# The last block's window units in another order, the samples' two in the middle, and the samples' norm on another engine

## Chip, cores and metric

One core of a Trainium2 chip runs the whole kernel. The metric is the device time of one execution in microseconds (us), the median of three runs. The engines are TensorE (PE, matmuls), VectorE (DVE), ScalarE (ACT) and GpSimd (POOL); SyncE (SP) issues DMAs from a queue that it works through in order, as every engine works through its own instructions in order.

## What is computed

One inference step of a two-layer encoder on a prompt of 1024 frames and 8 samples of 16 frames, width 1024. The parts that the change touches, cut from the reference:

```python
# layer 0: RWKV-7 time mixing, then a SwiGLU FFN; layer 1: attention, then a SwiGLU FFN
y, wkv_new = wkv7_scan(r, decay, k, v, -kk, kk * a_gate, wkv_prev)   # wkv_prev: the samples' states
y = (y - mu) * rsqrt(var + LNX_EPS) * ln_w + ln_b + bonus            # per head
out = (y * g) @ w_o                                                   # output projection
x = x + gate * out
h = rms_norm(x, g) * (1 + scale) + shift                              # before each FFN, K/V and Q
x = x + gate * (silu(h @ w_gate) * (h @ w_up)) @ w_down
```

`shift`, `scale` and `gate` are one vector for the prompt and one for each of the 8 samples ("modulations", themselves matmuls of the condition with a large weight).

## The kernel before

The 1152 columns (1024 prompt frames, 128 sample frames) are held as three blocks of 384. The scan runs by **windows** of 128 columns, 9 of them, and each window by two halves of the heads. One window and one half is a **unit**: number 12 is window 6, first half, 13 its second half, up to 17. Units 16 and 17 are window 8, which holds the samples; they start from the states read from memory (`ssv`, the tiles `sv` in the code, two buffers, one for each half of the samples) and write 16 new states back (`um`, `s2`, then a store). Units 12 to 15 carry the state `S` from window to window, so that 14 needs 12's result and 15 needs 13's; 16 and 17 need nothing of the others.

A unit has four steps: `win_prep` (loads `XL`, `BK`, `UV`, first products `G`), `win_run` (a chain of small matmuls: `st`, then `xs`, `TT`, then `Y`, which closes it), `win_post` (centre, variance, scale of `y`, ending in a store of the unit's `y` to the block `yg`), and a next unit's `win_prep`. `windows` runs the post of a unit beside the run of the next.

`outproj(b, c0, c1)` is the output projection of a column range of a block: it reads `yg` back (`mr`), splits it into a high and a low part (`mx` on ACT, the rest on DVE, line 255), does for each of 8 output tiles three matmuls per pair of tiles (24 matmuls `acc`, the weight `raw` also split into `whi` and `wlo`), adds the residual (`e`) and sums squares (`sqa`). Each matrix product in the kernel is done as these three matmuls. `outproj(2, 0, 256)` needs the units 12 to 15, `outproj(2, 256, 384)`, the samples' columns, the units 16 and 17. `ada` yields pieces of the modulations' product.

The program is written by Python generators: `alternate(a, b, m, n)` takes m steps of one and n of the other. A list scheduler then orders each engine's instructions, with the written order as priority.

After the last `outproj`, the first FFN begins (`S<-h,w`). It works in two column groups, c = 0 (512 prompt columns) and c = 1 (512 prompt and 128 sample columns). `strassen_in` loads the 8 tiles of a group, norms them (`normed`: DVE, line 326, and ACT, line 327), splits them (`h`) and forms sums of them on POOL (line 1230). The 128 sample columns are normed by `normed_samples`, three operations on a 128x128 tile, in four places: first FFN, K/V, Q, second FFN. The c = 0 part takes the memory that the units' pool frees (`cw.close()`).

Of the kernel before, what the change touches and what calls it, by code (L numbers as in the profile page):

```python
# [11 lines left out]
ALU = mybir.AluOpType  # L12
# [125 lines left out]
def mm(nc, out, lhsT, rhs, start, stop):  # L138
    return nc.tensor.matmul(out, lhsT, rhs, start=start, stop=stop)  # L139


class Trunk:
# [186 lines left out]
    def normed_samples(self, t, x, r, A, sh0, f):  # L329
        nc = self.nc  # L330
        tv = t.rearrange("p (b n) -> p b n", b=8)
        bc = lambda v: v[:, 1:9].rearrange("p (b o) -> p b o", o=1).broadcast_to([128, 8, 16])
        gp = nc.gpsimd
        gp.tensor_tensor(t, x, r, ALU.mult)
        gp.tensor_tensor(tv, tv, bc(A[:, f]), ALU.mult)
        gp.tensor_tensor(tv, tv, bc(self.mod[:, sh0 + f]), ALU.add)


    def proj_open(self, ctx):
# [364 lines left out]
    def win_open(self, ctx):  # L704
        nc = self.nc
        self.wp = ctx.enter_context(self.tc.tile_pool(name="win", bufs=1, reuse_waits="tile"))

        self.T = self.wp.tile([128, 16, 16], F32, name="T")
        nc.sync.dma_start(self.T.rearrange("p c i -> p (c i)"), self.a["ti"])
        self.Z = [self.dp.tile([64, 32, 64], F32, name=f"Z{i}") for i in range(2)]  # L710
        z = self.wt("y", [128, 512])
        nc.gpsimd.memset(z, 0.0)
        for i in range(2):
            zf = self.Z[i].rearrange("c g i -> (c g i)").rearrange("(u p x) -> u p x", u=2, p=128)
            for u in range(2):
                nc.sync.dma_start(zf[u], z)
        flat = lambda t: t.rearrange("p a b c d -> p (a b c d)")
        self.early = [lambda: flat(self.wt("YL", [128, 2, 2, 4, 64], 2))] * 2 + \
            [lambda: self.wt("BKT", [128, 2, 2, 256], 2).rearrange("p a b c -> p (a b c)")] * 2 + \
            [lambda: self.wt("XL", [128, 3, 8, 64], 2).rearrange("p a b c -> p (a b c)")] * 2 + \  # L720
            [lambda: self.wt("BK", [128, 8, 2, 64], 1).rearrange("p a b c -> p (a b c)"),
             lambda: self.wt("pa", [128, 2, 8, 64], 1).rearrange("p a b c -> p (a b c)")]
        self.zr = self.wp.tile([128, 128], F32R, name="zr")
        nc.scalar.activation(self.zr, z[:, 0:128], AF.Copy)
        self.eends = [self.wp.tile([128, 8, 12], F32, name=f"eend{b}") for b in range(NB)]
        self.S = []
        for h in range(2):
            s = self.wp.tile([128, 4, 64], F32, tag=f"S{h}", name=self.nm("S"), bufs=3)
            nc.gpsimd.memset(s, 0.0)
            self.S.append(s)  # L730
# [276 lines left out]
    def win_post(self, w, hf, R):  # L1007

        nc = self.nc
        b, wi = divmod(w, 3)  # L1010
        fs = slice(4 * hf, 4 * hf + 4)
        gt = self.wt("gl", [128, 512], 1)
        nc.sync.dma_start(gt.rearrange("p (f t) -> p f t", f=4), self.sp[b]["g"][:, wi, fs, :])
        bv = self.wt("bv", [128, 512], 1)
        nc.sync.dma_start(bv.rearrange("p (f t) -> p f t", f=4), self.sp[b]["v"][:, wi, fs, :])
        bn = self.wt("bn", [128, 512], 1)
        nc.sync.dma_start(bn.rearrange("p (f t) -> p f t", f=4), self.sp[b]["bn"][:, wi, fs, :])
        nc.gpsimd.tensor_tensor(bv, bv, bn, ALU.mult)
        y = self.wt("y", [128, 512], 1)
        nc.scalar.activation(y, R.Y, AF.Copy)  # L1020
        cen = self.bank("st", 2)
        mm(nc, cen, self.C("cen"), y, True, True)
        nc.scalar.activation(y, cen, AF.Square)
        yield
        var = self.bank("st", 2)
        mm(nc, var, self.C("bo"), y, True, True)
        nc.scalar.activation(y, var, AF.Ln, bias=self.eps[:, 1:2], scale=1.0 / 64)
        nc.scalar.activation(y, y, AF.Exp, scale=-0.5)
        nc.vector.tensor_tensor(y, cen, y, ALU.mult)
        yield  # L1030
        for f in range(4):
            s = slice(f * 128, (f + 1) * 128)
            nc.vector.scalar_tensor_tensor(y[:, s], y[:, s], self.P("lnw", 4 * hf + f), bv[:, s], ALU.mult, ALU.add)
        for f in range(4):
            s = slice(f * 128, (f + 1) * 128)
            nc.vector.scalar_tensor_tensor(y[:, s], y[:, s], self.P("lnb", 4 * hf + f), gt[:, s], ALU.add, ALU.mult)
        nc.scalar.dma_start(self.yg[b][:, fs, wi * 128:(wi + 1) * 128], y.rearrange("p (f t) -> p f t", f=4))

    @staticmethod
    def weave(*gens):  # L1040
# [100 lines left out]
    def layer0a(self, ctx):  # L1141
        self.yg = [self.dp.tile([128, 8, TB], F32, name=f"yg{b}") for b in range(NB)]
        c1, cw, ct = ExitStack(), ExitStack(), ExitStack()
        self.ps = c1.enter_context(self.tc.tile_pool(name="psA", bufs=1, space=PSUM, reuse_waits="tile"))
        self.win_open(cw)
        with ExitStack() as c2:
            self.proj_open(c2)
            for _ in self.proj(0):
                pass
            for b in range(1, NB):  # L1150
                w = self.windows([(w, hf) for w in range(3 * b - 3, 3 * b) for hf in range(2)])
                for _ in self.alternate(w, self.proj(b), 5, 4):
                    pass
        self.tail_open(ct)
        self.nraw, self.nhi, self.nlo = (2, 2, 2)
        self.nmix, self.nmr = 16, 2

        def ada():
            while next(self.ada, StopIteration) is not StopIteration:
                yield  # L1160

        def early():
            for b in range(2):
                yield from self.outproj(b)
        units = lambda t: self.windows([divmod(int(x), 2) for x in t.split()])
        for _ in self.alternate(units("12 13 14 15"), self.alternate(ada(), early()), 1, 1):
            pass
        for _ in self.alternate(units("16 17"), self.outproj(2, 0, 256), 3, 1):
            pass
        cw.close()  # L1170
        for _ in self.outproj(2, 256, 384):
            pass
        ct.push(c1)
        return ct.close
# [740 lines left out]
```

## Time and profile before

| | |
|---|---|
| median of three runs | 3966.8 us (3949.72, 3966.8, 3968.19) |
| profiled execution | 3959.5 us |
| its span, first to last instruction | 3957.6 us (1.9 us lie around it) |
| mean granted TensorE clock | 0.924 of full speed |
| PE busy | 3572.2 us, 90% of the span |
| DVE, ACT, POOL busy | 58%, 40%, 18% of the span |

The span is the time from the first to the last instruction in the trace; all times below count from its start. The profiled execution is 7.3 us under the median. A granted clock of 1.00 is 2.4 GHz, of 0.50 is 1.2 GHz; a stretch between them spent a part of its time at either.

### The profile page before, as it was taken

What the parts mean: (1) busy time and instruction counts of PE and PEld (TensorE: products, weight loads), DVE (VectorE), ACT (ScalarE), POOL (GpSimd) and SP (SyncE); (2) the same over time, 40 slices, a digit from 0 to 9 for tenths busy, and PEclk for the clock granted to TensorE, in tenths of its full rate; (3) what the DMA queues carried; (4) which work ended last, traced back from release to release, by engine and by line L of the source; (5) the groups of instructions that cost most, each with busy time, mean ns of one, the idle gap of its engine ahead of it and who ended that gap; (6) DMA issues with size and microseconds to landing.
All of it is one profiled execution on the core that took longest, in us unless ns stands there. A gap on an engine that the chain in (4) does not pass through costs nothing. (4 is left out here: it accounts for less than half of the span.)

```text
span 3957.6 us, 72834 instructions
## 1 busy us (share of the span) xinstructions
PE 3572.2 (90%) x28814; PEld 3153.8 (80%) x28814; DVE 2284.7 (58%) x4263; ACT 1586.3 (40%) x2994; POOL 708.6 (18%) x635
## 2 busy tenths in 40 slices
PE   6878998888887889999999999888889789999999
PEld 4766776776775679999988888777677789999998
DVE  4475575475554575455455852566676665545567
ACT  5554565363322343333321253455554443333310
POOL 0110110020000065454200200100000265444000
PEclk8888898798887769999999999999999889999999
DMA  5785685668764422222655313254464422222522
GB/s 201 216 246 141 178 243 163 177 182 234 216 161 123 139 76 84 73 73 75 216 204 189 105 62 100 81 165 147 142 199 148 160 68 73 75 75 91 172 79 73
DMA packets 439478, 556.56 MB, mean 141 GB/s; under 512 B 128864, under 2 KB 304224, under 8 KB 434656
## 3 DMA queue, kind: packets, MB, share of 16 engines
q1 hardware_dynamic: 384992, 533.01, 43.1%
q10 hardware_dynamic: 54144, 18.89, 2.1%
q8 instruction: 227, 3.72, 0.4%
q14 instruction: 115, 0.94, 0.1%
HBM read 417.63 MB, written 134.12 MB: 139 GB/s over the span
## 5 line engine op out<-in xcount | busy, mean ns | idle before, releaser
L139 PE MATMUL S<-h,w 128*128 128x320 f32 (+1 forms) x4944 | 695.5, 300 | 12.2 <-DVE h L255 3.1
L139 PEld LDWEIGHTS S<-h,w 128*128 128x128 f32 x4944 | 676.1, 193 | 18.6 <-DVE h L255 7.0
L139 PE MATMUL acc<-mx,whi 128*128 128x384 f32 (+2 forms) x1856 | 558.1, 382 | 63.9 <-ACT mx L254 31.1
L139 PE MATMUL S<-h,wh 128*128 128x320 f32 (+1 forms) x2844 | 532.0, 338 | 12.0 <-DVE h L1107 5.7
L139 PEld LDWEIGHTS S<-h,wh 128*128 128x128 f32 x2844 | 457.0, 190 | 68.4 <-issue 12.6
L139 PEld LDWEIGHTS acc<-mx,whi 128*128 128x128 f32 x1856 | 386.3, 223 | 99.7 <-ACT mx L254 36.1
L254 ACT ACTIVATE w<-rq 128x512 fp32r<-128x512 f32 x308 | 192.2, 629 | 499.4 <-PE S L139 199.6
L255 DVE TENSOR_TENSOR w<-rq,w 128x512 fp32r<-128x512 f32 x308 | 270.9, 883 | 200.5 <-ACT w L254 199.1
L139 PE MATMUL PT<-h,w 128*128 128x320 f32 (+1 forms) x2448 | 354.0, 300 | 16.7 <-ACT w L254 6.3
L139 PE MATMUL acc<-mx,wlo 128*128 128x384 f32 (+2 forms) x928 | 347.0, 375 | 7.1 <-DVE wlo L255 7.0
L139 PEld LDWEIGHTS PT<-h,w 128*128 128x128 f32 x2448 | 336.7, 193 | 20.7 <-ACT w L254 6.5
L139 PE MATMUL PT<-h,wh 128*128 128x320 f32 (+1 forms) x1428 | 288.5, 345 | 8.6 <-DVE wh L255 3.9
L1300 POOL TENSOR_TENSOR t<-t,t 128x576 f32<-128x576 f32 (+1 forms) x132 | 214.9, 1628 | 414.6 <-ACT t L1307 295.7
L139 PEld LDWEIGHTS PT<-h,wh 128*128 128x128 f32 x1428 | 235.2, 191 | 38.3 <-issue 8.8
L255 DVE TENSOR_TENSOR wlo<-raw,whi 128x1024 fp32r<-128x1024 f32 x116 | 146.1, 1262 | 127.3 <-ACT whi L254 126.3
L139 PEld LDWEIGHTS acc<-mx,wlo 128*128 128x128 f32 x928 | 205.0, 221 | 15.9 <-DVE wlo L255 9.1
L254 ACT ACTIVATE whi<-raw 128x1024 fp32r<-128x1024 f32 x116 | 121.8, 1053 | 143.2 <-PE acc L139 82.2
L255 DVE TENSOR_TENSOR h<-h,h 128x1024 fp32r<-128x1024 f32 (+4 forms) x112 | 123.3, 1115 | 85.5 <-ACT h L254 70.6
L254 ACT ACTIVATE h<-h 128x1024 fp32r<-128x1024 f32 (+4 forms) x112 | 103.2, 934 | 166.6 <-DMA h<-sd 114.8
L254 ACT ACTIVATE wh<-rq 128x512 fp32r<-128x512 f32 x124 | 74.6, 625 | 230.8 <-PE S L139 145.0
L1300 DVE TENSOR_TENSOR t<-S,t 128x576 f32<-128x576 f32 (+1 forms) x116 | 86.4, 744 | 129.9 <-PE S L139 129.8
L1367 DVE TENSOR_TENSOR h<-h,S 128x640 f32<-128x640 f32 (+1 forms) x150 | 112.0, 750 | 79.7 <-PE S L139 79.3
(424 smaller groups left out, 5748.8 us busy)
## 6 DMA issues: line engine op xcount, KB each, us to landing
h<-in_wada SPq DMA_DIRECT2D x64, 512.0 KB, 6.0
rq<-in_wg SPq DMA_DIRECT2D x88, 256.0 KB, 2.6
rq<-in_wu SPq DMA_DIRECT2D x88, 256.0 KB, 2.6
rq<-in_wd SPq DMA_DIRECT2D x88, 256.0 KB, 3.0
raw<-in_wada SPq DMA_DIRECT2D x32, 512.0 KB, 5.0
raw<-in_rw_o SPq DMA_DIRECT2D x32, 512.0 KB, 4.3
kc<-in_ck SPq DMA_DIRECT2D x16, 1024.0 KB, 5.1
vc<-in_cv SPq DMA_DIRECT2D x16, 1024.0 KB, 5.9
```

The source lines that it names most:

```text
L139: return nc.tensor.matmul(out, lhsT, rhs, start=start, stop=stop)
L254: self.nc.scalar.activation(hi, x, AF.Copy)
L255: self.nc.vector.tensor_tensor(lo, x, hi, ALU.subtract)
L1300: eng.tensor_tensor(out, x, y, ALU.add)
L1367: nc.vector.tensor_tensor(y, y, d, ALU.add)
```

## The change

Three things are edited. `layer0a` runs all six units from one generator, in the order 12, 13, 16, 14, 15, 17 instead of 12, 13, 14, 15 and then 16, 17. Beside it, in the ratio two steps of units to one, run the modulations and the projections, now with `outproj(2, 0, 256)` at their end; a set `posted`, which `win_post` fills, holds that back until unit 15's post has been written. And `normed_samples` issues its three operations on VectorE instead of GpSimd (8 tiles in 4 places, 96 instructions).

```diff
-        gp = nc.gpsimd
-        gp.tensor_tensor(t, x, r, ALU.mult)
-        gp.tensor_tensor(tv, tv, bc(A[:, f]), ALU.mult)
-        gp.tensor_tensor(tv, tv, bc(self.mod[:, sh0 + f]), ALU.add)
+        dve = nc.vector
+        dve.tensor_tensor(t, x, r, ALU.mult)
+        dve.tensor_tensor(tv, tv, bc(A[:, f]), ALU.mult)
+        dve.tensor_tensor(tv, tv, bc(self.mod[:, sh0 + f]), ALU.add)
...
+        self.posted = set()
...
         nc.scalar.dma_start(self.yg[b][:, fs, wi * 128:(wi + 1) * 128], y.rearrange("p (f t) -> p f t", f=4))
+        self.posted.add((w, hf))
...
         def early():
             for b in range(2):
                 yield from self.outproj(b)
-        units = lambda t: self.windows([divmod(int(x), 2) for x in t.split()])
-        for _ in self.alternate(units("12 13 14 15"), self.alternate(ada(), early()), 1, 1):
-            pass
-        for _ in self.alternate(units("16 17"), self.outproj(2, 0, 256), 3, 1):
+            while (7, 1) not in self.posted:
+                yield
+            yield from self.outproj(2, 0, 256)
+        w = self.windows([divmod(int(x), 2) for x in "12 13 16 14 15 17".split()])
+        for _ in self.alternate(w, self.alternate(ada(), early()), 2, 1):
             pass
         cw.close()
         for _ in self.outproj(2, 256, 384):
```

How the instructions stand is shown at three places. The number behind a name is that of the buffer's allocation; a row is line, operation, output<-inputs, shape, repeats.

**TensorE, where unit 16 closes.** Before, the closing products `Y_12990` of unit 16 are followed by the projection `outproj(2, 0, 256)` (`acc_13078`, then four more tiles; 115 of its matmuls stand there, up to unit 17's first `ssv` product):

```order
L139 MATMUL Y_12990<-XL_12592,ssv_12658 64x16 x23
L139 MATMUL st_12896<-um_12897,BKT_12630 64x256
L139 MATMUL Y_12990<-XL_12592,ssv_12658 64x16 x3
L139 MATMUL st_12896<-um_12900,BKT_12630 64x256
L139 MATMUL Y_12990<-XL_12592,ssv_12658 64x16 x3
L139 MATMUL acc_13078<-mx_12777,whi_13074 128x256
L139 MATMUL acc_13078<-mx_12778,whi_13074 128x256
L139 MATMUL acc_13078<-mx_12777,wlo_13075 128x256
```

Of the change, unit 16 (`Y_11867`) closes into the first products of unit 15 (`G`, from `XL_12243`) and the start of unit 14 (`Y_12209`):

```order
L139 MATMUL Y_11867<-XL_11477,ssv_11543 64x16 x12
L139 MATMUL st_11767<-um_11768,BKT_11515 64x256
L139 MATMUL Y_11867<-XL_11477,ssv_11543 64x16 x2
L139 MATMUL G_12254<-XL_12243,BK_12244 128x128 x3
L139 MATMUL st_11767<-um_11771,BKT_11515 64x256
L139 MATMUL G_12254<-XL_12243,BK_12244 128x128
L139 MATMUL G_12267<-XL_12243,BK_12244 128x128 x4
L139 MATMUL st_11778<-um_11779,BKT_11515 64x256
L139 MATMUL Y_12209<-zr 128x512
L139 MATMUL st_11778<-um_11782,BKT_11515 64x256
```

The state updates `um` of unit 16 now stand among other units' work. No `acc` row stands between unit 13's start and unit 17's first `ssv` products: block 1's projection ends ahead of them, and `outproj(2, 0, 256)` begins inside unit 17, with 94 of its 192 matmuls behind the post of unit 17.

**SyncE's queue, the samples' states of unit 17.** Before, the two loads `ssv` stand among unit 16's eight stores `out_wkv_s`, the first behind the sixth of them, the second behind the seventh:

```order
L946 DMA out_wkv_s<-s_2173_12925 128x256
L1133 DMA rr_13601<-in_x 128x256
L247 DMA raw_13674<-in_rw_o 128x1024
L998 DMA ssv_13175<-in_wkv 128x4x256
L946 DMA out_wkv_s<-s_2184_12975 128x256
L1136 DMA x_108<-e_2261_13460 128x256
L1133 DMA rr_13666<-in_x 128x256
L247 DMA raw_13772<-in_rw_o 128x1024
L998 DMA ssv_13177<-in_wkv 128x4x256
```

Of the change, they come behind the last of those stores, beside unit 15's loads of `UV`:

```order
L947 DMA out_wkv_s<-s_1956_11813 128x256
L826 DMA UV_12302<-sp_v_107 64x256 x3
L947 DMA out_wkv_s<-s_1960_11824 128x256
L826 DMA UV_12302<-sp_v_107 64x256
L791 DMA BK_12589<-sp_b_90 64x8x64
L999 DMA ssv_12658<-in_wkv 128x4x256
L999 DMA ssv_12660<-in_wkv 128x4x256
```

In the program's order two units, 14 and 15, now lie between these loads' place and unit 17.

**VectorE, behind unit 17's post.** Before, the four late low parts `mx` of the samples' columns (from `mr_13750` on) stand among the first norm operations of the FFN's c = 0 part (line 326):

```order
L1036 SCALAR_TENSOR_TENSOR y_13616<-y_13616,par,gl_13609 128x128 x4
L255 TENSOR_TENSOR mx_13749<-mr_13750,mx_13748 128x128
L255 TENSOR_TENSOR mx_13755<-mr_13756,mx_13754 128x128
L326 SCALAR_TENSOR_TENSOR x_14112<-x_14112,mod,x_14111 128x512
L326 SCALAR_TENSOR_TENSOR x_14113<-x_14113,mod,x_14111 128x512
L255 TENSOR_TENSOR mx_13761<-mr_13762,mx_13760 128x128
L326 SCALAR_TENSOR_TENSOR x_14114<-x_14114,mod,x_14111 128x512
L326 SCALAR_TENSOR_TENSOR x_14115<-x_14115,mod,x_14111 128x512
L255 TENSOR_TENSOR h_14122<-x_14112,h_14121 128x256
L255 TENSOR_TENSOR mx_13767<-mr_13768,mx_13766 128x128
```

Of the change, the same four stand at the end of that part, 57 rows and more behind its first norm operation, among its last splits (`h`, `w`):

```order
L255 TENSOR_TENSOR w_14261<-rq_14231,w_14260 128x512
L255 TENSOR_TENSOR h_14128<-x_14119,h_14127 128x256
L255 TENSOR_TENSOR mx_13749<-mr_13750,mx_13748 128x128
L255 TENSOR_TENSOR w_14265<-rq_14235,w_14264 128x512
L255 TENSOR_TENSOR mx_13755<-mr_13756,mx_13754 128x128
L255 TENSOR_TENSOR w_14269<-rq_14237,w_14268 128x512
L306 SCALAR_TENSOR_TENSOR kk_13716<-aux_13713,kk_13716 128x256
L255 TENSOR_TENSOR mx_13761<-mr_13762,mx_13760 128x128
L307 SCALAR_TENSOR_TENSOR rms_13715<-kk_13716,rms_13715 128x256
L255 TENSOR_TENSOR mx_13767<-mr_13768,mx_13766 128x128
```

The samples' projection has 168 matmuls behind the first of these four: half of its first two tiles and the six others whole.

## Rows read from the trace of the kernel before

**Rows 1.** The page's parts 1 and 2: busy time; granted clock in 40 slices (tenths).

```profile
PE 3572.2 (90%) x28814; PEld 3153.8 (80%) x28814; DVE 2284.7 (58%) x4263; ACT 1586.3 (40%) x2994; POOL 708.6 (18%) x635
...
PEclk8888898798887769999999999999999889999999
```

**Rows 2.** Stretches of 50 us: busy us of each engine, granted clock, DMA share, GB/s.

```profile
1150.00:1200.00 50.00, 40.06 (x448) 28.83 (x444) 23.40 (x57) 16.09 (x32) 2.55 (x2) 0.88 0.63 168
1200.00:1250.00 50.00, 36.77 (x375) 29.41 (x376) 16.37 (x40) 12.00 (x22) 1.26 (x1) 0.70 0.45 135
...
1350.00:1400.00 50.00, 30.54 (x128) 27.20 (x126) 37.57 (x73) 25.95 (x58) 17.32 (x16) 0.56 0.44 137
1400.00:1450.00 50.00, 37.42 (x181) 32.56 (x181) 33.48 (x57) 22.41 (x49) 27.48 (x36) 0.67 0.29 95
```

**Rows 3.** Timeline of PE, units 13 to 15: start, us, names, times, idle before.

```profile
1175.25 1.97 PE L139 MATMUL Y<-XL,S 64*64 64x64 f32 x32
...
1205.94 1.15 PE L139 MATMUL Y<-XL,S 64*64 64x64 f32 x32
...
1218.85 0.48 PE L139 MATMUL Y<-YL,UV 128*64 128x64 f32 x2 [4.88 <-DVE UV L931]
...
1245.44 1.15 PE L139 MATMUL Y<-XL,S 64*64 64x64 f32 x32
```

**Rows 4.** Timeline of PE, units 16 and 17.

```profile
1262.82 0.80 PE L139 MATMUL acc<-mx,whi 128*128 128x256 f32 x2 [4.93 <-ACT mx L254]
...
1280.64 0.82 PE L139 MATMUL Y<-XL,ssv 64*64 64x16 f32 x6
...
1302.83 0.42 PE L139 MATMUL st<-ssv,xm 64*32 64x64 f32 x8
...
1333.35 1.03 PE L139 MATMUL Y<-XL,ssv 64*64 64x16 f32 x8
```

**Rows 5.** Timeline of SP's queue, the samples' states for unit 17.

```profile
1300.60 0.38 SPq L998 DMA_DIRECT2D ssv<-in_wkv  x1
```

**Rows 6.** Timeline of ACT, unit 17's store.

```profile
1357.46 0.37 ACTq L1037 DMA_DIRECT2D yg<-y  x1
```

**Rows 7.** Timeline of PE from unit 17's store to the FFN.

```profile
1361.98 0.91 PE L139 MATMUL acc<-mx,whi 128*128 128x128 f32 x3 [8.95 <-ACT mx L254]
...
1413.88 0.80 PE L139 MATMUL aux<-sqa,cst 128*128 128x128 f32 x2 [1.43 <-DVE sqa L284]
1416.24 5.07 PE L139 MATMUL S<-h,w 128*128 128x256 f32 x24 [1.56 <-DVE kk L306]
```

**Rows 8.** PE by form, 1360 to 1415: count, busy us, mean ns, idle before.

```profile
L139 PE MATMUL acc<-mx,whi 128*128 128x128 f32 x112 | 35.8, 418 | 15.3 <-ACT mx L254 10.9 <-DVE e L1111 3.7 <-DVE mx L255 0.7
L139 PE MATMUL acc<-mx,wlo 128*128 128x128 f32 x56 | 23.2, 419 | 5.7 <-DVE wlo L255 5.7
```

**Rows 9.** Timeline of DVE after unit 17's store.

```profile
1364.22 0.75 DVE L326 SCALAR_TENSOR_TENSOR x<-x,mod,x 128x512 f32<-128x512 f32 x1 [1.36 <-DMA x<-x]
...
1404.05 0.67 DVE L255 TENSOR_TENSOR w<-rq,w 128x512 fp32r<-128x512 f32 x1
```

**Rows 10.** POOL, line 334: count, ns min/median/max, first and last start.

```profile
L334 POOL TENSOR_TENSOR xm<-h,rms x16: 458/870/912, 2261.3 to 2528.1; 128x128 f32<-128x128 f32 x16
```

**Rows 11.** DVE by form, 1400 to 1470.

```profile
L255 DVE TENSOR_TENSOR h<-x,h 128x320 fp32r<-128x320 f32 x28 | 27.5, 1030 | 2.8 <-ACT h L254 2.8
...
L1300 DVE TENSOR_TENSOR t<-PT,t 128x320 f32<-128x320 f32 x2 | 1.0, 482 | 0.0
L1111 DVE TENSOR_TENSOR e<-acc,mod 128x128 f32<-128x128 f32 x3 | 0.9, 285 | 4.2 <-PE acc L139 4.2
```

**Rows 12.** Stretches of 50 us at the shared K/V and the second FFN.

```profile
2250.00:2300.00 50.00, 42.38 (x188) 34.55 (x187) 41.69 (x60) 22.91 (x45) 23.75 (x30) 0.90 0.20 72
...
3150.00:3200.00 50.00, 30.82 (x142) 27.58 (x143) 43.20 (x57) 26.68 (x56) 37.29 (x43) 0.66 0.28 96
```

## The prediction

> **What bounds the kernel now.** I read the page first. TensorE is busy for 90% of the span, and its granted clock is 0.8 to 0.9 in many slices [rows 1]. So time can be won where TensorE waits or runs below full clock, and both of that is seen best in the stretches of 50 us: in the tail of the first layer, from 1150 to 1450, it is busy 31 to 40 us of each 50 that are shown, at a clock of 0.56 to 0.88, while DVE and ACT are far from full but for 1350 to 1400, where DVE is busy for 37.6 us [rows 2]. TensorE there waits for chains, not for a full engine.
>
> Then I followed the chain in the order of time. The closing products of the units end at 1177.2 (13), 1207.1 (14), 1246.6 (15), 1281.5 (16) and 1334.4 (17) [rows 3, 4]: intervals of 29.9, 39.5, 34.9 and 52.9 us. Three things lengthen them. Unit 15 falls into the stretch 1200 to 1250, in which TensorE idles 13.2 us [rows 2], 4.88 of it in a single wait [rows 3]. In unit 16 TensorE stands 4.93 us at a projection matmul whose input is unit 15's output, read back and split [rows 4]; the unit's own products queue behind it. And unit 17 begins only at 1302.83, 21.3 us after unit 16 closed [rows 4], because the second load of its states was issued at 1300.60 [rows 5], when unit 16's last updates had given the buffer back. TensorE is not idle in that gap: the projection of the first 256 columns fills it.
>
> Behind unit 17 comes a tail that nothing fills. Its output is stored at 1357.46 [rows 6]; 8.95 us of waiting for the read-back; then the samples' projection alone, and the FFN's first product starts at 1416.24 [rows 7], 58.8 us after the store. Of that, 168 matmuls take from 1361.98 to 1412.45 (the aux row less its wait [rows 7]), 50.5 us; taking off the waits of [rows 8] without the first (15.3 + 5.7 - 8.95 = 12.0) leaves 38.4 us, 0.23 each, at a granted clock of 0.56 [rows 2], nearly all at 1.2 GHz.
>
> **The order of the units, first part: up to unit 17's store.** Up to unit 13's end nothing is removed, so I start at 1177.2. Every unit then stands without a projection beside it until unit 17.
> - Unit 16: 34.9 less the 4.93 of its wait and some 24 projection matmuls gives 24 to 26; I take 28, with its ends at 24 and 35, because chain waits that a projection had filled stay.
> - Unit 14: 29.9 as it stands, some of it modulations; 28 (26 to 31). Unit 16's state updates overlap with it.
> - Unit 15: 39.5 less the 13.2 of idle time, which the projections' weight loads share the stretch with; 26 (24 to 30).
> - Unit 17: from 1302.83 to 1334.4 it took 31.6 with two dozen projection matmuls inside; it keeps as many; 31 (27 to 33). Its states are loaded two units ahead, so the gap of 21.3 us is gone.
> - Post: 1357.46 - 1334.4 = 23.1 [rows 4, 6]; more projection lies between; 24 (22 to 26).
>
> The sum is 1177.2 + 28 + 28 + 26 + 31 + 24 = 1314, against 1357.5: **43 us earlier** (25 to 57).
>
> **Second part: from the store to the FFN.** Here the change pays. Before, `outproj(2, 0, 256)` was done by then. Now 94 of its matmuls follow, and the samples' last four inputs are split on DVE at the end of the FFN's c = 0 norm and splits. That DVE block has its own length: from the store it ran through its first norm at 1364.22 to its last split, which ended at 1404.7 [rows 9], 47.3 us. The same rows must run now, with the projection's own splits among them as before, so the last input stands ready at about 47 us (45 to 50), and the 94 matmuls fit beside it. Behind it, 168 matmuls: 38.4 us at the lower level as measured, 19 at twice the clock. DVE is free by then and they can run densely, so I take 28. From the last matmul to the FFN's first product it took 1416.24 - 1412.45 = 3.8 [rows 7]. In all 47 + 28 + 3.8 = 79 us (68 to 92), against 58.8: **20 us paid back** (9 to 33). The 168 are the same number as in the old tail; the difference is that then they ran beside the DVE block, and now half behind it.
>
> Together: -43 + 20 = **-23 us**, with ends at 1300 + 68 = 1368 (-48) and 1332 + 92 = 1424 (+8).
>
> **The clock.** Same 32 closing products take 1.97 us in unit 13 and 1.15 in units 14 and 15 [rows 3]: the small matmuls do run at either level, and what stands beside a unit decides. The Trainium skill ("TensorE: Matmul & The Clock Gate", section "HAM oscillation — how this bites in real kernels") says that a TensorE which alternates between short bursts and waits falls back to its lower clock, and asks for matmuls to be kept together; by it taking the projections away from 16, 14 and 15 is the wrong direction, and the upper ends above would be the time. The trace agrees in part: unit 13 ran at the lower level though modulations stood beside it.
>
> **The norm of the samples' columns.** 24 operations in each of four places leave POOL and come to DVE. On POOL one took 0.46 to 0.91 us [rows 10]. On DVE the same shape takes 0.285 [rows 11], in all 6.8 us a place. Beside POOL, DVE is slower: a 128x320 split with both inputs in its memory took 1.03 us in the stretch where POOL works, against 0.48 for one with an input from PSUM [rows 11], a factor of 2.1; so up to 0.6 us, 14.4 a place. The Trainium skill ("SBUF — State Buffer", section "Who interferes with whom") has a rule for it: a DVE operation with two SBUF inputs and a POOL operation that reads SBUF shut each other out; the rows agree, and by it the moved operations cost the upper price wherever POOL's sums run beside them.
> What it hides behind: in the first FFN's stretch DVE has 16.5 us free of 50 [rows 2], at the second FFN 6.8, at K/V 8.3 [rows 12]; Q lies in a stretch where TensorE is nearly full. For POOL it is relief: its sums (line 1230), which the later splits wait for, come up to 24 operations earlier. At K/V and the second FFN, DVE goes over its free time by at most 6.1 + 7.6 us. Against that stand the 19.2 us that TensorE idles in the second FFN's stretch, some of which earlier sums may give back. I take 0, with ends -8 and +10. The scheduler also moves some attention work; no engine's amount changes, and I count nothing.
>
> **The rivals.**
> - *The clock comes back.* Dense matmuls behind the last input run at the upper level (19 us) and the units take their lower ends: -48. For it: unit 14 and 15's closing products at full speed; against: the old tail at 0.56. 3966.8 - 48 = 3919. Chance 0.25.
> - *The bare units and the tail stay at 1.2 GHz.* Upper ends: store at 1332, 79 to 85 more: 1411 to 1417, so -5 to +1, about 3964. For it: 0.56 and 0.67 in [rows 2]. Chance 0.26.
> - *The norm makes it slower.* All 96 operations at 0.6 us are 58 us of DVE. TensorE pays where DVE is the last to deliver, and DVE is at 41.7 and 43.2 of 50 at two of the four places [rows 12]. It decides the sign when more than 43 us of the 58 lie on the path (23 to eat the gain, 20 beyond); with all 58, -23 + 58 = +35, about 4002. Against it: free DVE time at the first FFN and at Q. Chance 0.14.
> - That the reorder does nothing because the scheduler undoes it: the order of the instructions excludes it.
>
> **How the numbers follow.** The forecast, chance 0.35: 3959.5 - 23 = 3936.5 on the profiled execution, and 7.3 more on the median, 3944; its own range is -36 to -10, 3931 to 3957. A measurement of this kernel tells about 0.5%, 20 us, from no change: faster is under 3947, slower over 3987. Faster: the first rival and some six tenths of the forecast, 0.25 + 0.21 = 0.46. Slower: the third, 0.14. The same: the second and the rest of the forecast, 0.26 + 0.14 = 0.40. The range for 8 in 10 leaves out the slower rival and a few in a hundred below: from -50 with the norm's -3 to the second rival with the norm's +10 and some more, 3914 to 3980.
>
> **What would show it.** In the profile after: unit 17's store near 1314 (under 1300 or over 1332 breaks the first part); no gap between a unit's close and the next unit's first products; unit 17's state loads issued a unit earlier; the FFN's first product near 1393, and TensorE waiting in the samples' projection for DVE's `mx`, 40 us and more after the store. If it doesn't wait there, the second part is wrong. The granted clock between 1177 and 1290 says which of the first two rivals holds. For the norm: TensorE's idle time in the four stretches against now, and the start of POOL's sums. The prediction is wrong as a whole if unit 15 or 17 waits for a load behind unit 16's stores in SP's queue, or if the change in the tail is given back in the FFN.

## The result, and the profile after

| | before | after |
|---|---|---|
| median, 12 runs each, side by side | 3955.05 us | 3975.99 us |
| lowest to highest | 3949.0 to 3968.45 | 3969.36 to 3984.86 |
| profiled execution | 3959.5 us | 3977.51 us |

The ratio is 1.0048, with a 95% interval of 1.0033 to 1.0064: the change makes the kernel slower by 19 us (13 to 25), just inside the 0.5% that the prediction calls "the same", but clear of zero, and on the other side of the forecast of 23 us faster. The measured 3975.99 us does lie in the range that the prediction gave, 3914 to 3980, but by luck: that range was counted from 3966.8, a median of three runs, and the 12 runs side by side with the change give 3955.05.

The page of the kernel after, its first two parts (busy time of each engine, then the span in 40 slices, in tenths):

```profile
span 3975.7 us, 72851 instructions
...
PE 3585.0 (90%) x28814; PEld 3152.8 (79%) x28814; DVE 2297.2 (58%) x4359; ACT 1588.0 (40%) x2994; POOL 658.7 (17%) x539
...
PE   6878888888898789999999999888889799999999
...
PEclk8988998798886769999999999989999889999999
```

The 96 norm instructions have gone from POOL to DVE. The counts say nothing about the loss, so the reading goes to the stretch that the order touches, cut at the closes of the units. After, one row for each of unit 16, 14, 15, 17, then unit 17's post up to its store, then from the store to the FFN's first product:

```profile
core 0: us, PE busy (x) PEld busy (x) DVE busy (x) ACT busy (x) POOL busy (x), PEclk, DMA share, GB/s
1172.50:1218.40 45.90, 42.63 (x448) 28.67 (x446) 15.56 (x41) 7.35 (x14) 1.27 (x1) 0.69 0.27 76
1218.40:1261.30 42.90, 38.15 (x274) 27.10 (x274) 19.41 (x50) 8.08 (x16) 1.27 (x1) 0.50 0.34 99
1261.30:1277.10 15.80, 11.01 (x168) 8.23 (x168) 4.29 (x13) 4.87 (x10) 1.26 (x1) 0.87 0.35 97
1277.10:1310.50 33.40, 30.87 (x393) 23.20 (x393) 11.25 (x29) 5.58 (x12) 1.27 (x1) 0.79 0.15 43
1310.50:1339.70 29.20, 25.21 (x142) 16.67 (x142) 19.23 (x47) 9.84 (x17) 0.00 (x0) 0.83 0.56 167
1339.70:1426.20 86.50, 61.14 (x292) 56.71 (x292) 52.68 (x101) 36.54 (x80) 20.09 (x16) 0.56 0.43 142
sum 253.70, PE 209.01 PEld 160.58 DVE 122.42 ACT 72.26 POOL 25.15; mean PE 34.83 PEld 26.76 DVE 20.40 ACT 12.04 POOL 4.19
```

The same windows of the kernel before, cut in the same way from the closes in [rows 3, 4] and the store in [rows 6]: units 14, 15, 16, the gap ahead of unit 17, unit 17, its post, and the way to the FFN:

```profile
1177.20:1207.10 29.90, 23.79 (x267) 17.16 (x267) 12.79 (x32) 8.06 (x16) 1.26 (x1) 0.81 0.55 155
1207.10:1246.60 39.50, 26.91 (x267) 21.82 (x267) 13.92 (x34) 10.23 (x19) 1.26 (x1) 0.70 0.45 130
1246.60:1281.50 34.90, 28.15 (x425) 21.11 (x425) 20.17 (x46) 9.51 (x18) 1.26 (x1) 0.84 0.40 114
1281.50:1302.80 21.30, 21.30 (x132) 17.01 (x132) 13.02 (x27) 6.09 (x9) 0.00 (x0) 0.94 0.50 158
1302.80:1334.40 31.60, 30.25 (x399) 23.15 (x399) 13.47 (x33) 7.36 (x14) 1.26 (x1) 0.85 0.41 128
1334.40:1357.50 23.10, 16.84 (x50) 8.65 (x50) 12.03 (x35) 3.63 (x8) 0.00 (x0) 0.65 0.17 52
1357.50:1416.20 58.70, 39.17 (x170) 37.10 (x170) 42.28 (x82) 28.10 (x64) 17.32 (x16) 0.50 0.38 119
sum 239.00, PE 186.41 PEld 146.00 DVE 127.68 ACT 72.98 POOL 22.37; mean PE 26.63 PEld 20.86 DVE 18.24 ACT 10.43 POOL 3.20
```

Read the two sums first. From unit 13's close to the FFN, 239.0 us have become 253.7, 14.7 us more. The two profiled executions are 18 us apart; -4.7 us lie ahead of unit 13's close and +8.1 us behind the FFN's first product. Among the other traces here both of these parts scatter by more than that: where the work ahead of it is left alone, unit 13 closes at 1170 to 1191 us, and the part behind takes 2536 to 2550 us. TensorE's idle time fell, from 52.6 to 44.7 us, as the reorder promises; but its busy time rose by 22.6 us, for 1717 matmuls against 1710. The matmuls became slower, and the column PEclk fell with them: units 16, 14 and 15 now take 91.8 us of TensorE for 890 matmuls, at 0.69, 0.50 and 0.87; before, the three units 14 to 16 took 78.9 us for 959, at 0.81, 0.70 and 0.84. Unit 14's stretch is at 0.50 from end to end, the lower level, while TensorE is busy 38 of its 43 us.

The timeline of TensorE after, at the closes of units 13, 14 and 15 (start, duration, what):

```profile
1170.55 1.97 PE L139 MATMUL Y<-XL,S 64*64 64x64 f32 x32
...
1259.33 1.97 PE L139 MATMUL Y<-XL,S 64*64 64x64 f32 x32
...
1275.99 1.15 PE L139 MATMUL Y<-XL,S 64*64 64x64 f32 x32
1277.07 0.42 PE L139 MATMUL st<-ssv,xm 64*32 64x64 f32 x8
```

Unit 14's 32 closing products now take 1.97 us; before they took 1.15 [rows 3]. The last two rows also show a step that came true: unit 17 starts on its states in the moment in which unit 15 closes, and the gap of [rows 4] is gone.

Behind unit 17's post, first the store (ACT's queue) and then four rows of TensorE's timeline, with idle time and releaser in brackets:

```profile
1339.66 0.37 ACTq L1038 DMA_DIRECT2D yg<-y  x1
...
1379.48 0.48 PE L139 MATMUL acc<-mx,whi 128*128 128x128 f32 x1 [2.66 <-DVE mx L255]
...
1385.38 0.48 PE L139 MATMUL acc<-mx,whi 128*128 128x128 f32 x1 [3.09 <-DVE mx L255]
...
1423.87 0.79 PE L139 MATMUL aux<-sqa,cst 128*128 128x128 f32 x2 [1.44 <-DVE sqa L284]
1426.22 2.04 PE L139 MATMUL S<-h,w 128*128 128x256 f32 x8 [1.56 <-DVE kk L306]
```

The samples' projection waits for DVE's `mx` 40 and 46 us after the store, as foretold; the last `mx` ends 48.9 us after it (DVE's row):

```profile
1388.29 0.29 DVE L255 TENSOR_TENSOR mx<-mr,mx 128x128 fp32r<-128x128 f32 x1
```

From there the rest of the projection runs to 1422.4, about 34 us.

### The profile page after: what moved, and what is told of

The parts are those of the page before. It is cut to its first block, busy times and chain, and to the rows that moved or that the text cites. A ratio compares the mean times of both kernels' runs of the same rounds, so it can differ in the third digit from the quotient of the medians.

```text
span 3975.7 us, 72851 instructions
## 1 busy us (share of the span) xinstructions
PE 3585.0 (90%) x28814; PEld 3152.8 (79%) x28814; DVE 2297.2 (58%) x4359; ACT 1588.0 (40%) x2994; POOL 658.7 (17%) x539
## 4 chain that ended last, share of the span: by engine, by line
PE 66%; DMA 12%; DVE 9%; ACT 5%; issue 3%; ACTq 1%; SPq 1%; POOL 1%; DVEq 0%; POOLq 0%
PE S L139 31%; PE PT L139 15%; PE acc L139 10%; PE st L139 3%; PE O L139 2%; DVE h L255 2%; PE PT L1744 1%; PE G L139 1%; DMA TT<-Z 1%; DVE wlo L255 1%; DMA rr<-sf_cs 1%; DMA vf<-in_wo 1%; DMA sp_b<-ag 1%; ACT whi L254 1%; PE Y L139 1%
## 5 line engine op out<-in xcount | busy, mean ns | idle before, releaser
L139 PE MATMUL acc<-mx,whi 128*128 128x384 f32 (+2 forms) x1856 | 547.1, 376 | 65.3 <-ACT mx L254 20.0
L1303 DVE TENSOR_TENSOR t<-S,t 128x576 f32<-128x576 f32 (+1 forms) x116 | 86.5, 746 | 135.2 <-PE S L139 135.1
L1370 DVE TENSOR_TENSOR h<-h,S 128x640 f32<-128x640 f32 (+1 forms) x150 | 112.0, 751 | 78.7 <-PE S L139 78.3
```

The lines of the kernel that those rows point to most:

```text
L1303: eng.tensor_tensor(out, x, y, ALU.add)
L1370: nc.vector.tensor_tensor(y, y, d, ALU.add)
```

## The experiments

Ratios are against the kernel before on the same chip, with 95% intervals; microseconds worked out from them use its median there, 3965.6 to 3969.2.

**One part alone: the order.** The kernel after with the norm on GpSimd again.

```diff
-        dve = nc.vector
-        dve.tensor_tensor(t, x, r, ALU.mult)
...
+        gp = nc.gpsimd
+        gp.tensor_tensor(t, x, r, ALU.mult)
...
```

> The new order of the units with the samples' norm left on GpSimd. If the order is the cause (units without a projection beside them, and the projection done behind them), the first FFN begins near 1426 us as in the changed kernel, 10 us later than before, the K/V and second FFN parts are as before, and the time is about 10 us over the kernel before (ratio 1.002 to 1.0035). If the norm on VectorE is the cause, the time is that of the kernel before, within 3 us, or faster.

Measured: 3979.21 against 3965.61 us, 1.0032 (1.0018 to 1.0046), 13 us slower (7 to 18). Its stretch from unit 13's close to the FFN is 251.2 us, like that of the kernel after. The order makes the greater part of the loss.

**The other part alone: the norm.** The kernel after with `layer0a` as before.

```diff
-            while (7, 1) not in self.posted:
-                yield
-            yield from self.outproj(2, 0, 256)
-        w = self.windows([divmod(int(x), 2) for x in "12 13 16 14 15 17".split()])
...
+        for _ in self.alternate(units("12 13 14 15"), self.alternate(ada(), early()), 1, 1):
+            pass
+        for _ in self.alternate(units("16 17"), self.outproj(2, 0, 256), 3, 1):
```

> The old order of the units with the samples' norm on VectorE. If the order is the main cause, this costs 3 to 9 us over the kernel before, most of it at the shared K/V (3 to 4 us) and the second FFN (1 to 2 us). If the norm is the main cause, it costs 15 to 21 us.

Measured: 3972.71 us, 1.0014 (0.9999 to 1.0029), 6 us slower (-0.4 to 11.5), which is not clear of nothing. The two parts add up to the whole, 13 + 6 against 19. This kernel also warns of single traces: its profiled execution, 3987.9 us, lay 15 over its median, and its stretch from unit 13's close to the FFN was 251.1 us in the old order. Its units 14 to 16 took 113.8 us at a mean granted clock of 0.71, where the trace of the kernel before has 104.3 us at 0.78. The verdict on the order rests on the many runs; the traces say where to look.

**One generator, plain order.** The kernel before with the new `early` and the ratio two to one, but the units in their old order and the norm on GpSimd.

```diff
+            while (7, 1) not in self.posted:
+                yield
+            yield from self.outproj(2, 0, 256)
+        w = self.windows([divmod(int(x), 2) for x in "12 13 14 15 16 17".split()])
+        for _ in self.alternate(w, self.alternate(ada(), early()), 2, 1):
```

> The new code with one generator and ratio two to one, norm on GpSimd, but the units in plain order 12 13 14 15 16 17. If the place of unit 16 is the cause, the projection of the first 256 columns lies beside units 16 and 17 again, unit 17 is stored near 1357 us, and the time is within 5 us of the kernel before. If it is the single generator, it is as slow as the new order, about 10 us over before.

Measured: 3967.87 us, 0.9997 (0.9979 to 1.0014); 179.9 us from unit 13's close to the store and 58.7 from there to the FFN, against 180.3 and 58.7 before. The ratio and the single generator cost nothing that these runs can see; this kernel and the one with the order alone differ in the string "12 13 16 14 15 17" only, and are 0.35% apart.

**A third buffer for the states.** The kernel before, with the gap of [rows 4, 5] shortened in another manner.

```diff
-            sv = self.st("ssv", [128, 4, 4, 64], 2)
+            sv = self.st("ssv", [128, 4, 4, 64], 3)
```

> The kernel before with a third buffer for the samples' states, so that the first half of unit 17's states loads early; nothing else. If the gap of 21 us between unit 16 and unit 17 was time lost, the time falls by 6 to 15 us. If the projection that fills it was work that had to be done anyway, it stays within 4 us.

Measured: 3957.02 against 3965.72 us, 0.9978 (0.9959 to 0.9998), 9 us faster (1 to 16). Unit 17 begins 15.9 us after unit 16 closes, from 1282.5 to 1298.4, where it was 21.3. So an earlier unit 17 does give time back, as long as the projection still stands beside the units.

**Late inputs at the end.** The kernel with the order alone, with the samples' inputs split into unused columns of the tiles that the block's first 256 columns hold, so that they need not wait for a free `mx` buffer.

```diff
-            h, l = self.mtile(w), self.mtile(w)
+            if own is None:
+                h, l = self.mtile(w), self.mtile(w)
+            else:
+                if len(own) <= f:
+                    own.append((self.mtile(), self.mtile()))
+                h, l = (t[:, c0:c1] for t in own[f])
```

> The new order, norm on GpSimd, and the samples' projection writes its split inputs into the free columns of the same 16 tiles that the first 256 columns use, so that the inputs need not wait for that projection's last product. If the late inputs are what stretches the part behind unit 17's store (86.6 us in the changed kernel), it falls to about 65 to 72 us and the time is 15 to 20 us under the order-only kernel. If TensorE at its lower clock is the bound there (286 matmuls at 0.21 us are 61 us, with waits some 80), it falls by less than 8 us.

Measured: 3965.0 against 3965.61 us, 1.0002 (0.9988 to 1.0016), some 12 us under the kernel with the order alone (the intervals lie apart by 0.02%). TensorE's projection matmuls behind the store, by form (count, busy us, mean ns, then idle time ahead of them and its releasers), first in the kernel after, then the narrow ones in this kernel:

```profile
L139 PE MATMUL acc<-mx,whi 128*128 128x128 f32 x128 | 41.8, 421 | 13.0 <-ACT whi L254 6.7 <-DVE mx L255 6.3
L139 PE MATMUL acc<-mx,wlo 128*128 128x128 f32 x64 | 26.4, 416 | 1.3 <-DVE wlo L255 1.3
L139 PE MATMUL acc<-mx,whi 128*128 128x256 f32 x48 | 12.5, 358 | 5.7 <-ACT whi L254 5.7
L139 PE MATMUL acc<-mx,wlo 128*128 128x256 f32 x24 | 9.2, 382 | 1.6 <-DVE wlo L255 1.6
```

```profile
L139 PE MATMUL acc<-mx,whi 128*128 128x128 f32 x128 | 38.3, 400 | 2.7 <-ACT whi L254 2.3 <-DVE e L1113 0.4
L139 PE MATMUL acc<-mx,wlo 128*128 128x128 f32 x64 | 25.6, 403 | 1.1 <-DVE wlo L255 1.1
```

The wait for DVE's `mx`, 6.3 us, is gone, and with it most of the wait for `whi` ahead of the narrow matmuls (ahead of the wide ones it is 7.2 us, where it was 5.7). The last `mx` ends 20.6 us after the store. From the store to the FFN it still takes 77.3 us, in a trace that is 16 us over this kernel's median, and more than expected: 96 projection matmuls that used to be done ahead of the store are now behind it (264, in the four forms of the kernel after, against 168), and at 0.21 us each (0.64 for three, in the timeline) they are 20 us, which with the old 58.7 makes 78.7. The late inputs are 9 to 12 us of the loss; the moved work is about the rest of what the second part costs.

**More work beside the bare units.** The order alone, with 36 products of 256 columns added, which nobody reads, behind each `xs` of units 16, 14 and 15.

```diff
+        if (w, hf) in ((7, 0), (7, 1), (8, 0)):
+            z = self.bank("st", 2)
+            for i in range(6):
+                mm(nc, z[:, 0:256], self.C("ident"), xs.rearrange("p f d -> p (f d)"), i == 0, i == 5)
```

> The order-only kernel with work added: behind each xs of the units 16, 14 and 15 stand six products of a 128x128 constant with a 128x256 tile, 36 in all, whose result nobody reads. At the upper clock they take 15 us, at the lower 31. If the small matmuls without a projection beside them let TensorE fall to its lower clock, and that is what makes the units long, the granted clock rises between unit 13's end and unit 15's end and that stretch (104.6 us in the changed kernel) grows by less than 8 us or shrinks. If the chain of waits makes them long, it grows by 15 to 31 us and the time with it.

Measured: 3979.39 against 3965.72 us, 1.0039 (1.0019 to 1.0059), no different from the kernel with the order alone. In the trace the added products are 72 matmuls, 22.9 us. Units 16, 14 and 15 in the kernel with the order alone, and then in this one:

```profile
1179.00:1225.10 46.10, 42.55 (x446) 28.67 (x446) 15.56 (x41) 7.36 (x14) 1.26 (x1) 0.69 0.28 78
1225.10:1264.70 39.60, 33.91 (x273) 23.89 (x273) 19.20 (x50) 8.10 (x16) 1.27 (x1) 0.59 0.37 107
1264.70:1281.40 16.70, 11.89 (x169) 9.01 (x168) 4.35 (x14) 5.39 (x12) 1.27 (x1) 0.81 0.34 95
```

```profile
1175.00:1221.80 46.80, 44.88 (x472) 32.42 (x470) 13.11 (x35) 7.35 (x14) 0.00 (x0) 0.75 0.20 58
1221.80:1263.40 41.60, 33.79 (x300) 23.27 (x301) 22.04 (x57) 8.09 (x16) 2.54 (x2) 0.79 0.44 127
1263.40:1286.10 22.70, 17.73 (x192) 12.94 (x193) 5.05 (x15) 5.82 (x13) 1.26 (x1) 0.85 0.31 88
```

In unit 14's stretch TensorE did 27 matmuls more in the same busy time, 33.8 against 33.9 us, at 0.79 instead of 0.59. The three units together are 111.1 us against 102.4: 22.9 us of added work for 8.7 us of time, though the idle time is not smaller (14.7 against 14.1). So it was not filled up: without the added products TensorE is busy for 73.5 us instead of 88.4, some 15 us less for the same matmuls. In these two traces the clock, and not a wait, is what the bare units pay. The many runs agree on the clock. Its mean over the whole execution is 0.9209 with the order alone, against 0.9232 before on that chip (12 and 35 runs), and 0.9252 with the products added, against 0.9235 before (10 and 29 runs).

**The projection held beside the units.** The order alone, and one product that nobody reads behind each `xs`, this time written to the projection's own banks in PSUM, so that block 1's projection can't be pulled ahead of units 16, 14 and 15.

```diff
+        if (w, hf) in ((7, 0), (7, 1), (8, 0)):
+            mm(nc, self.bank("acc", 2)[:, 0:256], self.C("ident"), xs.rearrange("p f d -> p (f d)"), True, True)
```

> The order-only kernel with one small product added behind each xs of the units 16, 14 and 15, in the projection's own accumulation banks, so that the scheduler can no longer pull block 1's projection ahead of these units: its tiles now lie beside them, in the ratio that the code writes. If TensorE's clock is the cause, the granted clock beside these units rises over 0.8, the units cost little more with the projection inside than without, and the time falls 8 to 20 us under the order-only kernel. If the chain is the cause, the time changes by less than 5 us, since the same TensorE work only changes its place.

Measured: 3987.2 against 3965.72 us, 1.0048 (1.0026 to 1.0071): slower than before, where a gain over the order alone was expected (against its 1.0032 no loss is clear either). Units 16, 14, 15, 17, and then from the store to the FFN:

```profile
1138.90:1183.80 44.90, 44.90 (x453) 34.54 (x455) 16.04 (x38) 6.77 (x12) 1.27 (x1) 0.69 0.28 81
1183.80:1229.10 45.30, 40.24 (x377) 29.08 (x377) 26.74 (x66) 14.21 (x26) 1.37 (x1) 0.91 0.60 180
1229.10:1258.10 29.00, 25.23 (x241) 19.63 (x241) 12.84 (x28) 11.67 (x23) 1.27 (x1) 0.88 0.55 174
1258.10:1298.40 40.30, 40.30 (x456) 31.84 (x454) 16.43 (x34) 8.68 (x14) 1.27 (x1) 0.90 0.42 128
1340.20:1450.20 110.00, 82.89 (x425) 73.79 (x424) 60.69 (x117) 45.36 (x94) 17.93 (x16) 0.61 0.48 154
```

The clock came up as expected beside units 14, 15 and 17; beside unit 16 it stayed at 0.69. But a projection put beside the units fills their time, the store comes hardly earlier (1340.2, against 1344.3 with the order alone), and block 2's first 256 columns are pushed behind it: 425 matmuls there in 110 us, at 0.61, against 292 in 86. What the clock gave in the middle went at the end.

**Block 2's projection in one piece.** If narrow matmuls at the lower level behind the store are the price, the two pieces of 256 and 128 columns should not be apart. The order alone, with all 384 columns projected behind the units.

```diff
-            self.residual(0 if b == 2 and c0 else w, f, 16, o, x, pz)
+            self.residual(0 if b == 2 and c0 else min(w, 256) if b == 2 else w, f, 16, o, x, pz)
...
-            while (7, 1) not in self.posted:
-                yield
-            yield from self.outproj(2, 0, 256)
...
-        for _ in self.outproj(2, 256, 384):
+        for _ in self.outproj(2):
```

> The order-only kernel with block 2's projection in one piece of 384 columns behind all units, instead of 256 and 128. If what is paid behind unit 17 is TensorE's own time for 286 narrow matmuls, it now has 168 of 384 columns (29 us at the upper clock, 54 at the lower): the store to the FFN takes 50 to 70 us instead of 86, and the time is 15 to 35 us under the order-only kernel. If it is the late inputs and the FFN's own norm and splits on VectorE (47 us from the store), it falls to 75 to 85 and the time by less than 10 us.

Measured: 3943.82 against 3965.72 us, 0.9938 (0.9918 to 0.9957), 25 us faster than before (17 to 33). Behind the store, by form and then in windows:

```profile
L139 PE MATMUL acc<-mx,whi 128*128 128x384 f32 x112 | 36.1, 409 | 23.1 <-ACT mx L254 12.6 <-DVE e L1113 9.4 <-DVE h L255 1.1
L139 PE MATMUL acc<-mx,wlo 128*128 128x384 f32 x56 | 22.4, 404 | 1.4 <-DVE wlo L255 1.4
```

```profile
1171.40:1332.10 160.70, 132.56 (x1312) 91.45 (x1311) 62.98 (x164) 29.19 (x55) 6.72 (x4) 0.70 0.32 94
1332.10:1398.30 66.20, 41.25 (x170) 37.23 (x171) 48.17 (x90) 31.90 (x64) 19.64 (x16) 0.76 0.43 141
```

The same columns need 168 matmuls behind the store instead of 264, 41 us of TensorE instead of 61, and the clock there is 0.76. From unit 13's close to the FFN it takes 226.9 us. (The `residual` line only gives the samples' 128 columns their own gate within the wider tile.)

**Both edits under the merge.** Four kernels with the merge cover both orders and both engines for the norm, two on one chip and two on another, in crossed pairs. The plain order is the string "12 13 14 15 16 17"; all else is as in the diffs above.

> Block 2's projection in one piece as in the merged kernel, but the units in plain order 12 13 14 15 16 17, norm on GpSimd. If the samples in the middle do win once no narrow projection is paid behind unit 17, this is slower than the merged kernel with the new order by 8 to 25 us, because unit 17 waits for the states' buffers with nothing to fill the gap. If the merge alone is what wins, it is within 5 us of it.

> The merged kernel in the new order, with the samples' norm on VectorE. If the norm's cost is its own and adds to whatever the order costs, this is 3 to 8 us slower than the merged kernel, most of it at the shared K/V. If the norm costs only together with a late start of the FFN, it is within 2 us.

> The last block's projection merged into one piece, the units in the plain order 12 to 17, the norm on VectorE. Runs on one chip with the next kernel, which has the samples' units in the middle and the norm on GpSimd; with the earlier pair (plain order with GpSimd against middle with VectorE: 3950.1 and 3936.4) the four cover both choices of both edits. If order and norm each act as they did without the merge (order +13, norm +6), this kernel is 7 us faster than the next and the earlier pair should have been 19 apart the other way round, which it was not. If the merge turns the order into a gain of about 10 and the norm costs about 4, this one is 14 slower than the next. If the order gains 14 and the norm costs nothing, as the earlier pair alone would be read, this one is 14 slower too; then the difference of the two pairs is zero and so is the norm.

> Merged projection, the samples' units in the middle, the norm on GpSimd: the same program as the earlier merged kernel, beside the plain order with the norm on VectorE on one chip. It was 22 us faster than before then. Faster than the kernel with the plain order and VectorE by 14 to 18 if the order gains behind the merge and the norm costs 0 to 4; slower than it by some 7 if the order still loses.

| | plain order | samples' units in the middle |
|---|---|---|
| norm on GpSimd | 0.9951 (0.9932 to 0.9971) | 0.9934 (0.9910 to 0.9959) |
| norm on VectorE | 0.9959 (0.9947 to 0.9972) | 0.9919 (0.9897 to 0.9941) |

The medians are 3950.13 and 3940.23 us above, 3952.49 and 3936.36 below. If the two edits add up, half the sum of the two crossed differences (0.32% and 0.25%) is the order: a **gain** of 0.29%, 11 us, with some 8 us of uncertainty if the intervals' halves are added in squares. Half their difference is the norm: 0.04% in favour of VectorE, 1.4 us with the same uncertainty, so nothing that these runs can see. The best kernel has the new order, the norm on VectorE, and the merge: 32 us faster than before (23 to 41). Where the order's gain under the merge arises is not settled: from unit 13's close to the FFN the kernels with the plain order took 223.6 and 224.0 us, those with the new one 226.9, 218.8 and 221.7 (the first of them is the merged kernel above).

These five traces also answer whether it is the order itself that makes units long. None of them has a projection beside the units 14, 15 and 16. From unit 13's close to unit 17's first product they took 99.9 and 100.5 us in the plain order (13 us of it a gap ahead of unit 17) and 106.5, 99.2 and 104.4 us in the new one, and the mean granted clock of the three units was 0.67 to 0.70 in all five. So bare units cost about the same in either order: the miss lies in their being bare, and not in the order as such.

## Why the prediction was wrong

*The step that failed: first part, the terms for units 16 and 14.* I took 28 for unit 16 (24 to 35) and 28 for unit 14 (26 to 31); they took 45.9 and 42.9. The prediction said itself that "every unit then stands without a projection beside it until unit 17", and priced a unit without a projection as its old time less waits. Unit 15, whose work overlaps with unit 14's, took 15.8 instead of 26; the three make 104.6 against 82, and 22.6 us of the 30 by which the first part went wrong. (The other two traces of this order, with the norm on GpSimd and with the shared tiles, have 102.4 and 106.6.) The old windows of the three took 104.3 us: nothing was saved, although the projection and the modulations, which had kept TensorE busy for some 21 us beside them, had gone but for 4. Two things stand in the place of what was to be saved.

The first is the clock. The old times stood on 0.78 as a mean over the three units (0.71 in the trace with the norm alone, which has the same order); with the other work gone, the small matmuls of unit 14 ran at 0.50 throughout, where it had 0.81 with nothing but modulations beside it. By the products added beside them this is worth about 15 us, in a pair of single traces; the clocks of the many runs show the direction, not the price. The Trainium skill ("TensorE: Matmul & The Clock Gate", section "HAM oscillation — how this bites in real kernels") was on that side; the trace agrees with its direction, though in unit 14's stretch TensorE was not in short bursts between long waits but busy for 89% of it.

The second is work that the prediction put at nothing: "Unit 16's state updates overlap with it." Of these 32 matmuls, 16 stood in the old windows and 16 in the gap behind unit 16; now all stand in the three units. The rows are the old windows, the old gap, and the three units after:

```profile
L139 PE MATMUL st<-um,BKT 128*64 128x256 f32 x16 | 4.9, 463 | 0.0
```

```profile
L139 PE MATMUL st<-um,BKT 128*64 128x256 f32 x16 | 5.2, 405 | 0.0
```

```profile
L139 PE MATMUL st<-um,BKT 128*64 128x256 f32 x32 | 14.0, 627 | 1.8 <-DVE um L941 1.8
```

The 16 more are some 5 us at the old price. With the clock's 15 that makes about 20 of the 22.6 us. A misreading in the working was small: the 13.2 us of idle time taken off unit 15 belong to the stretch from 1200 to 1250; its own window has 12.6.

*Unit 17 and post.* 33.4 and 29.2 instead of 31 and 24: both over their ends (33 and 26), at 0.79 and 0.83. From unit 13's close to the store 167.2 us, where 137 were forecast and 180.3 stood before: 13 us earlier instead of 43.

*Second part.* The wait came where it was foretold, the sizes were low: the last `mx` at 48.9 us (47 forecast), the matmuls behind it in 34 us (28), 3.8 to the FFN (3.8), together 86.5 (79, with ends at 68 and 92). The forecast counted 168 matmuls behind the last `mx`; that is the number behind the first of the last four, and 154 were left behind the last. The 28 assumed a clock between the two levels; it was at the lower one, 0.50 from 1388.6 to 1424. 28 us paid back instead of 20. That 47 came so near is in part luck, since its reason, the length of DVE's block of norm and splits, was not what held the last inputs: there are 16 `mx` buffers, and the projection of the first 256 columns needs them all up to its last output tile. With free columns to go to, the last `mx` ended 20.6 us after the store beside the same block, and 9 to 12 us came back.

*Together* -13 + 28 = +15 us in place of -23 in the traces. In many runs the order costs 13.

*The norm.* Forecast 0 (-8 to +10); measured +6 (-0.4 to 11.5) beside the two pieces and -1 (8 either way) beside the merge. The 96 operations on DVE, for example these two forms of the kernel after,

```profile
L335 DVE TENSOR_TENSOR xm<-xm,mod 128x128 f32<-128x128 f32 x16 | 5.6, 353 | 0.0
L334 DVE TENSOR_TENSOR xm<-h,rms 128x128 f32<-128x128 f32 x16 | 4.6, 286 | 0.3 <-DMA out_v<-vt 0.2
```

took 28.7 us over all their forms, 0.30 each: the lower price (0.285), not the upper (0.6). Some 18 of them overlap in the trace with an operation on GpSimd, and three of these took longer: 1.37, 0.83 and 0.50 us. So the upper price was paid in single places, and not throughout a stretch in which GpSimd works, as the prediction had priced it. At K/V the move does show: from VectorE's first `xm` to the first product `O<-ht` it took 37.8 us before and 41.3 after, and the same 37 to 38 or 41 to 42 in every kernel here with one or the other. So the first product comes 3 to 4 us later there. In total I can't tell them from nothing.

*The rivals.* "The clock comes back" is refuted, for units and tail. "The bare units and the tail stay at 1.2 GHz" had the right direction, but its ends (155 us from unit 13's close to the store and at most 240 to the FFN, against 167 and 254) were still 12 and 14 us short, because I had taken them from units that ran with other work beside them, and had left the state updates out. "The norm makes it slower" had the right sign and, as far as the runs tell, the wrong price: not 58 us.

## What to carry to other kernels

A stretch that was moved away from other TensorE work did not keep its time less its waits here: look at the granted clock of the stretch, ask which work beside it kept the clock up, and price the stretch at the level that is left. When a gap is taken away, list everything that ran in it, small updates too. Filler work that is pulled out of a gap is not saved; look where it is done instead, how wide its matmuls are there and at which clock. A reorder's sign can depend on the next stage: the same order lost 13 us with the projection in two pieces behind it and gained some 11 (8 either way) with it in one.

## What the hardware showed that I had not expected

At the lower level a matmul of 128 columns took as long as one of 256: behind the store, three of either took 0.64 us. Three rows of the timeline of the kernel after: two matmuls of 256 columns at 2.4 GHz, then two of 256 and two of 128 columns at 1.2 GHz:

```profile
1350.27 0.40 PE L139 MATMUL acc<-mx,whi 128*128 128x256 f32 x2
...
1359.08 0.63 PE L139 MATMUL acc<-mx,whi 128*128 128x256 f32 x2
...
1371.06 0.63 PE L139 MATMUL acc<-mx,whi 128*128 128x128 f32 x2
```

Splitting 384 columns into 256 and 128 thus costs two passes of 0.21 us there, where one pass of 384 took 0.32 (0.96 for three, from 1373.90 to 1374.86 in the merged kernel, at the lower level). And busy is not the same as clocked up: TensorE was busy for 38 of 43 us at exactly 0.50 in unit 14's stretch, while in the gap before unit 17, busy throughout with the projection, it had 0.94.
